# Hybrid MoBA / RWKV-7 layer on one core: GpSimd idle in the first stage, a fifth tile from the unnormed x, a shorter first chain step, a split last tile, a new tile order

## The chip, the cores and the metric

The kernel runs on 1 core of one Trainium2 chip. The metric is device microseconds of one execution: the median of 3 runs of the kernel before is 571.07 us (570.91 to 571.47).

## What is computed

One layer of a decoder trunk, in float32, for 512 tokens of width 1024. Cut to what matters here:

```python
u = rms_norm(x, g_pre)                 # x * rsqrt(mean(x*x) + 1e-6) * g_pre, a factor per token
cols = u @ w_in                        # 49 tiles of 128 columns: q k v z of branch A, r k v z of branch B,
                                       # decay and in-context-rate inputs, 16 tiles of two merge gates
y_a = block_attention(q, k, v, rel_bias) * silu(z_A)
state = 0                              # branch B, per head a 64x64 state; a scan over the tokens
state = state * w_t + (state @ a_t) b_t' + v_t k_t';  y_t = state @ r_t
y_b = (group_norm(y) + bonus) * silu(z_B)
merged = sigmoid(g_A) * (y_a @ p_a) + sigmoid(g_B) * (y_b @ p_b)
h = x + rms_norm(merged @ w_out, g_post)
out = h + sigmoid(h @ w_ple_gate) * (p @ w_ple_up)
```

The norm's factor belongs to a token, so a tile of `cols` may be made from x times g_pre and multiplied by the factor afterwards.

## The kernel before

Tokens lie along the free dimension (T = 512), features on the 128 partitions. A product "tile" is 128 output columns by 512 tokens: 8 blocks of the contraction, and for each block 3 matmuls (`product`, `mm3`), since both sides are split into a high and a low part: high by high, high weight by low activation, low weight by high activation. The high part is a rounding copy on ScalarE (ACT), the low part a subtraction on VectorE (DVE). So a tile is 24 matmuls on TensorE (PE) and, for its weights, one ACT copy `whi` and one DVE subtraction `wlo` of 128x1024. Two buffers hold split weights: a tile's weights can be split once the tile two places ahead has been multiplied.

**First stage.** x comes in four pieces of 128x1024 (two token halves h by two feature halves q), between them the weights of the first tiles. `x_split` makes `xh` (ACT) and `xl` (DVE) from x times g_pre, 128x256 at a time. `first_tiles` makes four tiles from these, before the norm is known: k0 and r0 (PSUM tiles named s) in the order k0 half 0, r0 half 0, k0 half 1, r0 half 1, then v0 (named y) and the tile of the decay and rate inputs (named c). `first_out` multiplies them by the norm's factor. Meanwhile `squares` sums x*x: half 0 on GpSimd (POOL), half 1 with ACT's Square and DVE's additions; `pre_norm` turns the sums (`rms`) into the factor by four one-column matmuls (g<-ones,rms), a short DVE sequence and four matmuls that spread it (g<-cst,rb); then it makes `uf` (DVE) for the 8 feature blocks, and `norm_split` makes `u_hi` (ACT) and `u_lo`, the latter on POOL or DVE, whichever the planner takes to be free earlier.

**Filling tiles.** The other 45 column tiles are made by `fill` from `u_hi` and `u_lo` in the order of the table FILL, into two PSUM buffers (pp); `evacuate` empties them in the same order. Between their matmuls a planner (`Plan.run`) places the work of branch B (`rwkv`, `inverse`, `chain`, `post`) and the attention. It keeps a modelled time for each engine, takes the engine whose next item can start first, and breaks ties by ranks (RC, RR_, RI, RP and so on). The instructions of each engine run in the order in which the planner issued them.

**The chain.** `chain(s)` steps 8 times (c = 0 to 7) through the state `SV` of two tiles of heads. A step's output in PSUM tile y is a product of `W2` with the step's new values plus, on top, a product of `W1` with the state. At c = 0 the state is zero (memset).

**The end.** `gate_out` multiplies h by `w_ple_gate`, 8 tiles w0 to w7; `gate_evac` takes each through ACT's Tanh and two DVE instructions to an output DMA. The last tile, w7, is made in two halves of 256 tokens, each in its own PSUM buffer.

Of the kernel before, what the change touches and what calls it, by code (L numbers as in the profile page):

```python
# [32 lines left out]
OP = mybir.AluOpType  # L33
# [8 lines left out]
GN_EPS = 64e-5  # L42
DECAY = math.exp(-0.5)
FILL = """
Z0 Q0 V0 r1 K0 v1 z0 g0 k1 g1 r2 g2 k2 g3 Q1 Z1 K1 z1 V1 g4 v2 r3 v3
g5 k3 V2 Z2 g6 K2 g7 Q2 g8 g9 g10 g11 V3 Z3 K3 Q3 z2 g12 z3 g13 g14 g15
"""

LAST = "o0 o1 o5 o2 o6 o3 o7 o4 w2 w0 w1 w3 w4 w5 w6 w7"
# [7 lines left out]
SQ = 0.1  # L57
SAME = 0.03
URGENT = 5
RC, RR_, RI, RP, RA, RE, RW = 10, 9, 6, 2, 8, 10, 11  # L60
WR, WA, WC = 0.0, 0.0, 0.0

VEC = {}
# [263 lines left out]
def hybrid_kernel(ctx: ExitStack, tc, xT, pT, wu, wda, wmain, wpab, wout, wpg, vec_in, cst_in, oneh, relb, wupa,  # L327
# [13 lines left out]
    def bank(tag="g", bufs=2):  # L341
        return psum.tile([128, 512], F32, tag=tag, name=tag, bufs=bufs)
# [87 lines left out]

    FULL = slice(0, T)
    HALF = slice(0, T // 2), slice(T // 2, T)

    def product(name, ps, mh, ml, kts, cols=FULL, done=True, pace=None):

# [269 lines left out]
    def squares(h, sq):  # L705

        for q in range(2):
            ks = slice(4 * q, 4 * q + 4)
            yield ("wait", f"dx{h}{q}")
            if h:  # L710
                yield "A"
                act.activation(sq[:, ks], x_sb[:, h, ks], AF.Square)
            else:
                yield "G"
                pool.tensor_tensor(sq[:, ks], x_sb[:, h, ks], x_sb[:, h, ks], op=OP.mult)
        e = dve if h else pool
        for w in (4, 2):
            yield e.key
            e.tensor_tensor(sq[:, 0:w], sq[:, 0:w], sq[:, w:2 * w], op=OP.add)
        yield e.key  # L720
        e.tensor_tensor(rms[:, HALF[h]], sq[:, 0], sq[:, 1], op=OP.add)
        plan.mark(f"sum{h}")

    def pre_norm():
# [34 lines left out]
    def norm_split(kt, uf):  # L759
        yield "A"  # L760
        act.activation(u_hi[:, kt, :], uf, AF.Copy)
        e = pool if plan.t["G"] + 0.7 < plan.t["D"] else dve
        yield e.key
        e.tensor_tensor(u_lo[:, kt, :], uf, u_hi[:, kt, :].bitcast(F32), op=OP.subtract)
        plan.mark(f"u{kt}")

    def bias_lines():
# [25 lines left out]
    def statics():  # L793

        nonlocal po_, rw, W1, W2, AT32, SV, Zm, reset
        for m in ["wa", "lines", "consts"] + [f"u{k}" for k in range(8)]:
            yield ("wait", m)
        start_stack.close()
        po_ = rw_stack.enter_context(tc.tile_pool(name="post", bufs=1))
        rw = chain_stack.enter_context(tc.tile_pool(name="rwkv", bufs=1))  # L800
        W1 = rw.tile([128, 2, NCH, 4, C], F32, name="W1")
        W2 = rw.tile([128, 2, NCH, 2, 128], F32, name="W2")
        AT32 = rw.tile([128, 2, NCH, 128], F32, name="AT32")
        SV = rw.tile([128, 2, NCH, 2, 2, C], F32, name="SV")
        Zm = [rw.tile([128, NCH, 128], F16, name=f"Z{i}") for i in range(5)]
        reset = rw.tile([128, NCH, 65], F16, name="reset")
        plan.mark("open")
        yield "G"
        pool.memset(reset, 1.0)
        pool.memset(reset[:, :, 0], 0.0)  # L810
        pool.memset(reset[:, :, 33], 0.0)
        plan.mark("reset")
        pool.memset(SV[lo_, :, 0, 0, 0, :], 0.0)
        pool.memset(SV[hi_, :, 0, 1, 0, :], 0.0)
        for p in range(2):
            pool.memset(W1[hi_, p, :, 1, :], 0.0)
# [9 lines left out]
    def fill(kinds):  # L826
        for i, (w, j) in enumerate(kinds):
            if w in "krv" and j >= BUFS[w + "b"]:
                yield ("wait", f"done{w}{j - BUFS[w + 'b']}")
            if w == "z":  # L830
                yield ("wait", f"post{j - 2}" if j >= 2 else "open")
            if w in "QKVZ":
                yield ("wait", f"attn{j - 1}" if j else "usedfirst2")
            if i >= 2:
                yield ("wait", f"ev{i - 2}")
            ps = bank("pp", 2)
            yield from product(f"{w}{j}", ps, u_hi, u_lo, K8, pace=lambda k: f"u{k}")
            plan.spawn(evacuate(i, w, j, ps), 0.0, RE)
        plan.mark("filled")

    def evacuate(i, w, j, ps):
        if i:
            yield ("wait", f"ev{i - 1}")
        yield "A"
        if w in "krv":
            d, off = {"k": (KK, 4), "r": (RR, 0), "v": (VV, 8)}[w]
            d[j] = krv.tile([128, T], F32, tag=w + "b", name=w + "b", bufs=BUFS[w + "b"])
            yield from shift_mix(ps, off + j, d[j])
        elif w == "z":
            z = tmp("z", "zt")  # L850
            yield from shift_mix(ps, 12 + j, z)
            th = ZZ[j] = po_.tile([128, T], F32, tag="zb", name="zb", bufs=2)
            yield "A"
            act.activation(th, z, AF.Tanh, scale=0.5)
            yield "D"
            dve.scalar_tensor_tensor(th, th, 1.0, z, op0=OP.add, op1=OP.mult)
        elif w == "Q":
            q = QS[j] = at.tile([128, 2, T], F32R, tag="qs", name="qs")
            for h, a, b in ((0, lo_, hi_), (1, hi_, lo_)):
                yield "A"  # L860
                act.activation(q[a, h, :], ps[a], AF.Copy, scale=-0.125)
                yield "D"
                dve.scalar_tensor_tensor(q[b, h, :], ps[a], -0.125, q[a, h, :].bitcast(F32), op0=OP.mult,
                                         op1=OP.subtract)
        elif w == "K":
            kh = KH[j] = at.tile([128, 2, T], F32R, tag="kh", name="kh")
            kl = KL[j] = at.tile([128, 2, T], F32R, tag="kl", name="kl")
            for h, a, b in ((0, lo_, hi_), (1, hi_, lo_)):
                yield "A"
                act.activation(kh[a, h, :], ps[a], AF.Copy)  # L870
                act.activation(kh[b, h, :], ps[a], AF.Copy)
                yield "D"
                dve.tensor_tensor(kl[a, h, :], ps[a], kh[a, h, :].bitcast(F32), op=OP.subtract)
                yield "A"
                act.activation(kl[b, h, :], kl[a, h, :].bitcast(F32), AF.Copy)
        elif w == "V":
            vc = tmp("vc", "zt")
            act.activation(vc, ps, AF.Copy)
            VT[j] = at.tile([128, 4, 128], F32, tag="vt", name="vt")
            yield "P"  # L880
            for tt in range(4):
                s = slice(tt * 128, tt * 128 + 128)
                pe.transpose(ps[:, s], vc[:, s], ident)
            yield "A"
            act.activation(VT[j].rearrange("p a b -> p (a b)"), ps, AF.Copy)
        elif w == "Z":
            th = ZA[j] = at.tile([128, T], F32, tag="za", name="za")
            act.activation(th, ps, AF.Tanh, scale=0.5)
            yield "D"
            dve.scalar_tensor_tensor(th, th, 1.0, ps, op0=OP.add, op1=OP.mult)  # L890
        elif w == "g":
            gs = at.tile([128, T], F32, tag="est", name="gst")
            act.activation(gs, ps, AF.Tanh, scale=0.5)
            sp.dma_start(g_dram[:, j, :], gs)
        plan.mark(f"ev{i}")
        plan.mark(f"{w}{j}")
# [282 lines left out]
    def chain(s):  # L1179
# [8 lines left out]
        for c in range(NCH):  # L1188
# [33 lines left out]
            if c % 4 == 0:  # L1222
                yb = bank("y", 1).rearrange("p (a c b) -> p a c b", a=2, b=C)
            for p in two:
                pe.matmul(yb[lo_, p, c % 4], W2[:, p, c, 0, 0:64], SV[:, p, c, 0, 1, :], start=True, stop=False)
                pe.matmul(yb[hi_, p, c % 4], W2[:, p, c, 1, 0:64], SV[:, p, c, 1, 1, :], start=True, stop=False)
                pe.matmul(yb[lo_, p, c % 4], W1[:, p, c, 1, :], SV[:, p, c, 0, 0, :], start=False, stop=True)
                pe.matmul(yb[hi_, p, c % 4], W1[:, p, c, 2, :], SV[:, p, c, 1, 0, :], start=False, stop=True)
            if c % 4 == 3:
                plan.spawn(outputs(s, c, yb, Y), 0.0, RR_, WR)  # L1230
            plan.cur.now = now
# [346 lines left out]
    def gate_out():  # L1578
# [14 lines left out]
            plan.spawn(gate_evac(n, FULL, ps[n]), 0.1)  # L1593
        for n in range(3, 8):
            yield ("wait", f"w{n - 4}" if n > 3 else "e3")
            for c in HALF if n == 7 else (FULL,):
                p = bank("g", 2) if n % 4 == 3 else bank(("c", "s0", "s1")[n % 4], 1)
                yield from product(f"w{n}", p, F["hi"], F["lo"], K8, c, c != HALF[0])
                plan.spawn(gate_evac(n, c, p), 0.1)

    def gate_evac(n, c, ps):
# [64 lines left out]
```

## Time and profile before

| | |
|---|---|
| median of 3 runs | 571.07 us |
| the profiled execution | 570.33 us |
| its span | 568.5 us |
| PE busy | 555.5 us, 98% of the span |
| PE weight load busy | 450.2 us, 79% |
| DVE busy | 418.1 us, 74% |
| ACT busy | 290.1 us, 51% |
| POOL busy | 18.3 us, 3% |
| chain that ended last | PE 84%, DVE 11%, ACT 2% |
| mean granted TensorE clock | 0.994 of full |

The span is from the first to the last instruction; the profiled execution's own time has 1.8 us around it. Times in rows count from the span's start. Matmuls overlap one another: the distance between two starts is what one costs in a stream, not its duration. A plain float32 matmul runs as two passes, and each pass is a record; the split products (float32r) have one.

### The profile page before, as it was taken

The numbers are of one execution on the slowest core, as the hardware profiler recorded it, in microseconds if no ns is written. First come the engines' busy times: TensorE is split into PE (matmuls) and PEld (weight loads), VectorE is DVE, ScalarE is ACT, GpSimd is POOL, SyncE is SP. The second block draws the span as 40 slices with busy tenths as digits, with TensorE's granted clock in tenths as the row PEclk, the third lists the DMA queues.
The fourth block names the chain that finished last, engine by engine and source line by source line (L and its number), as shares of the span: only waits on it lengthen the run. The fifth ranks groups of instructions, "written<-read, shape, count | busy, mean of one in ns | idle before, by whom it ended". The sixth has DMA issues, their size and how long they took to land.

```text
span 568.5 us, 10221 instructions
## 1 busy us (share of the span) xinstructions
PE 555.5 (98%) x3983; PEld 450.2 (79%) x3983; DVE 418.1 (74%) x922; ACT 290.1 (51%) x568; POOL 18.3 (3%) x26
## 2 busy tenths in 40 slices
PE   5999999999999999999999999999999999999997
PEld 2986788877777777777778777777888898999886
DVE  6988679799677777879988865589856666488623
ACT  7535683763355665464855434754533255543311
POOL 6121100000000000000000000000000000000000
PEclk9799999999999999999999999999999999999999
DMA  8322523123421204332222331124565557702201
GB/s 303 132 71 86 176 93 111 56 75 126 145 80 71 93 1 139 118 121 96 80 91 92 112 112 52 62 86 143 199 200 208 187 185 270 247 10 66 93 38 55
DMA packets 27704, 66.56 MB, mean 117 GB/s; under 512 B 2911, under 2 KB 7519, under 8 KB 27656
## 3 DMA queue, kind: packets, MB, share of 16 engines
q1 hardware_dynamic: 27656, 65.91, 34.0%
q8 instruction: 31, 0.51, 0.4%
q14 instruction: 17, 0.14, 0.1%
HBM read 56.71 MB, written 11.82 MB: 121 GB/s over the span
## 4 chain that ended last, share of the span: by engine, by line
PE 84%; DVE 11%; ACT 2%; issue 1%; DMA 1%; ACTq 0%; DVEq 0%; SPq 0%
PE pp L294 47%; PE s L294 14%; PE g L294 11%; PE c L294 7%; PE y L294 5%; DVE wlo L294 2%; DVE xl L294 1%; DVE u_lo L294 1%; DMA xg<-xT 1%; DMA yf<-yB_dram 1%; DVE uf L294 1%; DVE Ep L294 1%; DVE ts L294 0%; DVE var L294 0%; DVE h_lo L294 0%
## 5 line engine op out<-in xcount | busy, mean ns | idle before, releaser
L294 PE MATMUL pp<-u_hi,whi 128*128 128x512 f32 x360 | 145.9, 405 | 0.8 <-DVE za L294 0.6
L294 PE MATMUL pp<-u_lo,whi 128*128 128x512 f32 x360 | 145.0, 403 | 0.0
L294 PE MATMUL pp<-u_hi,wlo 128*128 128x512 f32 x360 | 144.6, 402 | 0.0
L294 ACT ACTIVATE whi<-raw 128x1024 fp32r<-128x1024 f32 (+1 forms) x86 | 71.5, 846 | 73.2 <-PE pp L294 55.4
L294 DVE TENSOR_TENSOR wlo<-raw,whi 128x1024 fp32r<-128x1024 f32 (+1 forms) x86 | 81.5, 960 | 25.1 <-ACT whi L294 24.6
L294 PEld LDWEIGHTS pp<-u_hi,whi 128*128 128x128 f32 x360 | 67.7, 188 | 15.2 <-issue 2.0
L294 PEld LDWEIGHTS pp<-u_lo,whi 128*128 128x128 f32 x360 | 67.8, 188 | 12.8 <-issue 0.6
L294 PEld LDWEIGHTS pp<-u_hi,wlo 128*128 128x128 f32 x360 | 67.8, 188 | 12.6 <-issue 0.2
L294 ACT ACTIVATE P<-P,sml 128x128 f32<-128x128 f32 (+3 forms) x32 | 17.7, 554 | 9.1 <-DVE sml L294 9.1
L294 DVE SCALAR_TENSOR_TENSOR SV<-c,D,sd 64x64 f32<-64x64 f32 x56 | 15.9, 283 | 8.2 <-PE c L294 6.7
L294 ACT ACTIVATE Xt<-y 128x512 f16<-128x512 f32 x20 | 11.9, 593 | 17.0 <-PE y L294 16.7
L294 ACT ACTIVATE sd<-SV,D 64x64 f32<-64x64 f32 x56 | 19.3, 344 | 1.1
L294 DVE TENSOR_TENSOR Z<-c,lvl 128x512 f16<-128x512 f32 x20 | 13.7, 687 | 5.4 <-PE c L294 5.3
L294 PEld LDWEIGHTS c<-SV,W 128*64 128x64 f32 x240 | 9.6, 136 | 9.7 <-issue 4.8
L294 PE MATMUL pp<-m_hi,whi 128*128 128x512 f32 (+1 forms) x48 | 17.0, 354 | 0.0
L294 PE MATMUL pp<-m_lo,whi 128*128 128x512 f32 (+1 forms) x48 | 17.0, 354 | 0.0
L294 PE MATMUL pp<-m_hi,wlo 128*128 128x512 f32 (+1 forms) x48 | 17.0, 354 | 0.0
L294 DVE SCALAR_TENSOR_TENSOR xl<-xg,xh 128x256 fp32r<-128x256 f32 x16 | 13.0, 876 | 5.0 <-ACT xh L294 5.0
L294 DVE CUSTOM_DVE_ANT_0 P<-s,bt 128x128 f32<-128x128 f32 (+3 forms) x32 | 14.4, 487 | 1.7 <-PE s L294 1.4
L294 DVE TENSOR_SCALAR SV<-c 64x128 f32<-64x128 f32 x30 | 8.6, 288 | 9.5 <-PE c L294 5.9
L294 PE MATMUL s<-xl,whi 128*128 128x256 f32 x32 | 10.8, 338 | 3.8 <-DVE xl L294 3.8
L294 DVE SCALAR_TENSOR_TENSOR t<-gb,pp 128x512 f32<-128x512 f32 (+1 forms) x8 | 5.2, 654 | 12.5 <-PE pp L294 12.5
(366 smaller groups left out, 1246.5 us busy)
## 6 DMA issues: line engine op xcount, KB each, us to landing
raw<-wmain SPq DMA_DIRECT2D x48, 512.0 KB, 3.3
g_dram<-gst SPq DMA_DIRECT2D x16, 256.0 KB, 2.0
raw<-wpab SPq DMA_DIRECT2D x8, 512.0 KB, 3.3
raw<-wout SPq DMA_DIRECT2D x8, 512.0 KB, 3.5
raw<-wpg SPq DMA_DIRECT2D x8, 512.0 KB, 5.8
bb_dram<-b_dram SPq DMA_DIRECT2D x4, 640.0 KB, 5.9
bt<-bb_dram SPq DMA_DIRECT2D x8, 256.0 KB, 3.6
ga<-g_dram SPq DMA_DIRECT2D x8, 256.0 KB, 3.8
```

The lines of the kernel that those rows point to most:

```text
L294: r = f(out, *args, **kw)
```

## The change

`squares` puts both halves on ACT (Square) and DVE (additions); `norm_split` puts every `u_lo` on DVE. POOL's first work after the start is now the memsets at 50-odd us. The first filling tile, g0, is made from `xh` and `xl`; its `evacuate` multiplies by the factor (`rms`) on DVE before the Tanh. The chain's first step leaves out the products with the zero state. The last tile goes in pieces of 256, 128 and 128 tokens, the two narrow ones in one PSUM buffer. FILL has a new order, RP goes from 2 to 7.

```diff
 FILL = """
-Z0 Q0 V0 r1 K0 v1 z0 g0 k1 g1 r2 g2 k2 g3 Q1 Z1 K1 z1 V1 g4 v2 r3 v3
-g5 k3 V2 Z2 g6 K2 g7 Q2 g8 g9 g10 g11 V3 Z3 K3 Q3 z2 g12 z3 g13 g14 g15
+g0 r1 Z0 Q0 V0 K0 z0 v1 g1 k1 z1 r2 g2 g3 k2 g4 Z1 K1 Q1 V1 v2 r3 v3
+g5 k3 V2 Z2 g6 K2 Q2 g7 g8 g9 g10 V3 K3 Q3 g11 Z3 z2 z3 g12 g13 g14 g15
 """
-RC, RR_, RI, RP, RA, RE, RW = 10, 9, 6, 2, 8, 10, 11
+RC, RR_, RI, RP, RA, RE, RW = 10, 9, 6, 7, 8, 10, 11
...
+    ENDS = HALF[0], slice(T // 2, 3 * T // 4), slice(3 * T // 4, T)
...
     def squares(h, sq):
         for q in range(2):
-            if h:
-                yield "A"
-                act.activation(sq[:, ks], x_sb[:, h, ks], AF.Square)
-            else:
-                yield "G"
-                pool.tensor_tensor(sq[:, ks], x_sb[:, h, ks], x_sb[:, h, ks], op=OP.mult)
-        e = dve if h else pool
+            yield "A"
+            act.activation(sq[:, ks], x_sb[:, h, ks], AF.Square)
         for w in (4, 2):
-            yield e.key
-            e.tensor_tensor(sq[:, 0:w], sq[:, 0:w], sq[:, w:2 * w], op=OP.add)
+            yield "D"
+            dve.tensor_tensor(sq[:, 0:w], sq[:, 0:w], sq[:, w:2 * w], op=OP.add)
...
     def norm_split(kt, uf):
-        e = pool if plan.t["G"] + 0.7 < plan.t["D"] else dve
-        yield e.key
-        e.tensor_tensor(u_lo[:, kt, :], uf, u_hi[:, kt, :].bitcast(F32), op=OP.subtract)
+        yield "D"
+        dve.tensor_tensor(u_lo[:, kt, :], uf, u_hi[:, kt, :].bitcast(F32), op=OP.subtract)
...
     def fill(kinds):
-            yield from product(f"{w}{j}", ps, u_hi, u_lo, K8, pace=lambda k: f"u{k}")
+            if i:
+                yield from product(f"{w}{j}", ps, u_hi, u_lo, K8, pace=lambda k: f"u{k}")
+            else:
+                yield ("wait", "usedfirst3")
+                yield from product(f"{w}{j}", ps, xh, xl, K8)
...
     def evacuate(i, w, j, ps):
+        else:
+            for k in range(6):
+                yield ("wait", f"u{k}")
+            gs = at.tile([128, T], F32, tag="est", name="gst")
+            yield "D"
+            dve.tensor_tensor(gs, ps, rms, op=OP.mult)
+            ps = gs
...
     def chain(s):
-                pe.matmul(yb[lo_, p, c % 4], W2[:, p, c, 0, 0:64], SV[:, p, c, 0, 1, :], start=True, stop=False)
-                pe.matmul(yb[hi_, p, c % 4], W2[:, p, c, 1, 0:64], SV[:, p, c, 1, 1, :], start=True, stop=False)
-                pe.matmul(yb[lo_, p, c % 4], W1[:, p, c, 1, :], SV[:, p, c, 0, 0, :], start=False, stop=True)
-                pe.matmul(yb[hi_, p, c % 4], W1[:, p, c, 2, :], SV[:, p, c, 1, 0, :], start=False, stop=True)
+                for rows, h in ((lo_, 0), (hi_, 1)):
+                    pe.matmul(yb[rows, p, c % 4], W2[:, p, c, h, 0:64], SV[:, p, c, h, 1, :], start=True, stop=c == 0)
+                for rows, h in ((lo_, 0), (hi_, 1)) if c else ():
+                    pe.matmul(yb[rows, p, c % 4], W1[:, p, c, 1 + h, :], SV[:, p, c, h, 0, :], start=False, stop=True)
...
     def gate_out():
-            for c in HALF if n == 7 else (FULL,):
-                p = bank("g", 2) if n % 4 == 3 else bank(("c", "s0", "s1")[n % 4], 1)
-                yield from product(f"w{n}", p, F["hi"], F["lo"], K8, c, c != HALF[0])
+            for c in ENDS if n == 7 else (FULL,):
+                if c != ENDS[2]:
+                    p = bank("g", 2) if n % 4 == 3 else bank(("c", "s0", "s1")[n % 4], 1)
+                yield from product(f"w{n}", p, F["hi"], F["lo"], K8, c, c.stop == T)
                 plan.spawn(gate_evac(n, c, p), 0.1)
```

What the change moves, at the three places that the prediction speaks of. First DVE, from the end of the small parameter preparations (`oka`) to the norm's first instruction (`ms4`); `sq` are the squared halves, `wlo` a low weight part. Before, then now:

```order
L294 TENSOR_SCALAR oka_79<-hka_78 128x4
L294 TENSOR_TENSOR sq_141<-sq_141 128x1024
L294 TENSOR_TENSOR sq_141<-sq_141 128x512
L294 TENSOR_TENSOR rms_113<-sq_141 128x256
L294 TENSOR_TENSOR wlo_306<-raw_225,whi_305 128x1024
L294 TENSOR_SCALAR ms4_368<-g_139 128x4
```

```order
L294 TENSOR_SCALAR oka_79<-hka_78 128x4
L294 TENSOR_TENSOR sq_140<-sq_140 128x1024
L294 TENSOR_TENSOR sq_140<-sq_140 128x512
L294 TENSOR_TENSOR rms_113<-sq_140 128x256
L294 TENSOR_TENSOR sq_141<-sq_141 128x1024
L294 TENSOR_TENSOR sq_141<-sq_141 128x512
L294 TENSOR_TENSOR rms_113<-sq_141 128x256
L294 TENSOR_TENSOR wlo_302<-raw_223,whi_301 128x1024
L294 TENSOR_SCALAR ms4_381<-g_139 128x4
```

Half 0's three additions have come to DVE, ahead of those of half 1.

Second PE, from the end of the fourth tile (c) into the first filling tile (pp). Before, then now:

```order
L294 MATMUL c<-xl,shi 128x512
L294 MATMUL c<-xh,slo 128x512
L294 MATMUL pp<-u_hi,whi 128x512 [waits Activation_49]
L294 MATMUL pp<-u_lo,whi 128x512 [waits Pool_49]
L294 MATMUL pp<-u_hi,wlo 128x512
```

```order
L294 MATMUL c<-xl,shi 128x512
L294 MATMUL c<-xh,slo 128x512
L294 MATMUL pp<-xh,whi 128x512 [waits Activation_49]
L294 MATMUL pp<-xl,whi 128x512
L294 MATMUL pp<-xh,wlo 128x512
```

The 24 matmuls behind the fourth tile read x instead of u; the first matmul that waits for u comes one tile later, and none waits for POOL.

Third PE, in the last tile (w7, in PSUM tile g). Before, its 48 matmuls are 256 wide up to the program's end; now 24 are so, and 48 are narrow. The end before; then, of the change, the place where the narrow ones begin, and the place where the third piece begins (its first matmul is the fourth row of the last fence):

```order
L294 MATMUL g<-h_lo,whi 128x256
L294 MATMUL g<-h_hi,wlo 128x256
L294 MATMUL g<-h_hi,whi 128x256
L294 MATMUL g<-h_lo,whi 128x256
L294 MATMUL g<-h_hi,wlo 128x256
L1661 UNCONDITIONAL_BRANCH
```

```order
L294 MATMUL g<-h_hi,whi 128x256
L294 MATMUL g<-h_lo,whi 128x256
L294 MATMUL g<-h_hi,wlo 128x256
L294 MATMUL g<-h_hi,whi 128x128
L294 MATMUL g<-h_lo,whi 128x128
L294 MATMUL g<-h_hi,wlo 128x128
```

```order
L294 MATMUL g<-h_hi,whi 128x128
L294 MATMUL g<-h_lo,whi 128x128
L294 MATMUL g<-h_hi,wlo 128x128
L294 MATMUL g<-h_hi,whi 128x128
L294 MATMUL g<-h_lo,whi 128x128
L294 MATMUL g<-h_hi,wlo 128x128 [waits Activation_49]
```

The number of matmuls in the last tile goes from 48 to 72, and its third piece has a wait for ACT at its third matmul.

## Rows read from the trace of the kernel before

**Rows 1.** Busy time by stretch: us, busy us (instructions) by engine, clock, DMA.
```profile
10.00:15.00 5.00, 1.63 (x6) 1.13 (x6) 5.00 (x3) 5.00 (x15) 4.77 (x3) 0.83 1.03 396
15.00:20.00 5.00, 4.73 (x21) 4.58 (x22) 5.00 (x13) 3.60 (x8) 0.79 (x1) 0.50 0.59 198
...
60.00:500.00 440.00, 439.12 (x3331) 352.31 (x3330) 330.22 (x737) 234.51 (x445) 0.00 (x0) 1.00 0.36 122
```

**Rows 2.** PE in order of time, first stage: start us, us, instruction.
```profile
6.57 0.38 PE L294 MATMUL s<-xh,whi 128*128 128x256 f32 x1 [0.37 <-ACT whi L294]
...
13.85 0.58 PE L294 MATMUL s<-xl,whi 128*128 128x256 f32 x1 [1.89 <-DVE xl L294]
...
26.64 0.28 PE L294 MATMUL s<-xl,whi 128*128 128x256 f32 x1
26.76 0.28 PE L294 MATMUL s<-xh,wlo 128*128 128x256 f32 x1
...
39.39 0.40 PE L294 MATMUL c<-xl,shi 128*128 128x512 f32 x1
39.62 0.39 PE L294 MATMUL c<-xh,slo 128*128 128x512 f32 x1
```

**Rows 3.** DVE in order of time, 9 to 40 us.
```profile
9.18 6.91 DVE L294 SCALAR_TENSOR_TENSOR xl<-xg,xh 128x256 fp32r<-128x256 f32 x4
...
17.35 3.25 DVE L294 SCALAR_TENSOR_TENSOR xl<-xg,xh 128x256 fp32r<-128x256 f32 x8
...
23.63 1.94 DVE L294 TENSOR_TENSOR sq<-sq 128x1024 f32<-128x1024 f32 x2
...
25.95 1.22 DVE L294 TENSOR_TENSOR wlo<-raw,whi 128x1024 fp32r<-128x1024 f32 x1
...
34.47 2.72 DVE L294 SCALAR_TENSOR_TENSOR uf<-xg,g 128x512 f32<-128x512 f32 x4 [0.38 <-PE g L294]
37.23 2.46 DVE L294 TENSOR_TENSOR u_lo<-uf,u_hi 128x512 fp32r<-128x512 f32 x2
```

**Rows 4.** ACT in order of time, 10 to 19 us.
```profile
10.96 3.29 ACT L294 ACTIVATE xh<-xg 128x256 fp32r<-128x256 f32 x8
...
16.60 2.00 ACT L294 ACTIVATE sq<-xg 128x1024 f32<-128x1024 f32 x2
```

**Rows 5.** POOL in order of time, 8 to 15 us.
```profile
8.17 2.84 POOL L294 TENSOR_TENSOR sq<-xg 128x1024 f32<-128x1024 f32 x1 [1.72 <-DMA xg<-xT]
11.09 3.85 POOL L294 TENSOR_TENSOR sq<-sq 128x1024 f32<-128x1024 f32 x2
```

**Rows 6.** PE, a stall behind DVE at 53 us.
```profile
53.19 0.47 PE L294 MATMUL pp<-u_hi,whi 128*128 128x512 f32 x1 [0.56 <-DVE za L294]
```

**Rows 7.** PE in a chain step: eight output matmuls (two passes each), then large ones.
```profile
359.57 0.64 PE L294 MATMUL y<-SV,W 128*64 128x64 f32 x16
360.13 0.50 PE L294 MATMUL pp<-u_hi,whi 128*128 128x512 f32 x1
360.47 0.39 PE L294 MATMUL pp<-u_lo,whi 128*128 128x512 f32 x1
```

**Rows 8.** PE, narrow matmuls: one column, then 128 columns.
```profile
28.97 0.95 PE L294 MATMUL g<-ones,rms 128*128 128x1 f32 x8
...
79.22 0.22 PE L294 MATMUL s<-kh,qs 128*128 128x128 f32 x1
79.28 0.27 PE L294 MATMUL s<-kl,qs 128*128 128x128 f32 x1
79.39 0.33 PE L294 MATMUL s<-kh,qs 128*128 128x256 f32 x1
```

**Rows 9.** The end on PE, ACT and DVE, last half tile.
```profile
564.10 0.28 PE L294 MATMUL g<-h_hi,wlo 128*128 128x256 f32 x1
...
564.41 0.38 ACT L294 ACTIVATE th<-g 128x256 f32<-128x256 f32 x1 [2.34 <-PE g L294]
...
565.28 0.42 DVE L294 SCALAR_TENSOR_TENSOR x_sb<-th,x_sb 128x256 f32<-128x256 f32 x1
```

More of the change, by code (lines that the diff above doesn't have):

```diff
@@ L709, in squares @@
             yield ("wait", f"dx{h}{q}")
-            if h:
-                yield "A"
-                act.activation(sq[:, ks], x_sb[:, h, ks], AF.Square)
-            else:
-                yield "G"
-                pool.tensor_tensor(sq[:, ks], x_sb[:, h, ks], x_sb[:, h, ks], op=OP.mult)
-        e = dve if h else pool
+            yield "A"
+            act.activation(sq[:, ks], x_sb[:, h, ks], AF.Square)
         for w in (4, 2):
-            yield e.key
-            e.tensor_tensor(sq[:, 0:w], sq[:, 0:w], sq[:, w:2 * w], op=OP.add)
-        yield e.key
-        e.tensor_tensor(rms[:, HALF[h]], sq[:, 0], sq[:, 1], op=OP.add)
+            yield "D"
+            dve.tensor_tensor(sq[:, 0:w], sq[:, 0:w], sq[:, w:2 * w], op=OP.add)
+        yield "D"
+        dve.tensor_tensor(rms[:, HALF[h]], sq[:, 0], sq[:, 1], op=OP.add)
         plan.mark(f"sum{h}")
@@ L761, in norm_split @@
         act.activation(u_hi[:, kt, :], uf, AF.Copy)
-        e = pool if plan.t["G"] + 0.7 < plan.t["D"] else dve
-        yield e.key
-        e.tensor_tensor(u_lo[:, kt, :], uf, u_hi[:, kt, :].bitcast(F32), op=OP.subtract)
+        yield "D"
+        dve.tensor_tensor(u_lo[:, kt, :], uf, u_hi[:, kt, :].bitcast(F32), op=OP.subtract)
         plan.mark(f"u{kt}")
@@ L795, in statics @@
         nonlocal po_, rw, W1, W2, AT32, SV, Zm, reset
-        for m in ["wa", "lines", "consts"] + [f"u{k}" for k in range(8)]:
+        for m in ["wa", "lines", "consts", "ev0"] + [f"u{k}" for k in range(8)]:
             yield ("wait", m)
@@ L843, in evacuate @@
             yield ("wait", f"ev{i - 1}")
+        else:
+            assert w == "g"
+            for k in range(6):
+                yield ("wait", f"u{k}")
+            gs = at.tile([128, T], F32, tag="est", name="gst")
+            yield "D"
+            dve.tensor_tensor(gs, ps, rms, op=OP.mult)
+            ps = gs
         yield "A"
@@ L891, in evacuate @@
         elif w == "g":
-            gs = at.tile([128, T], F32, tag="est", name="gst")
+            gs = at.tile([128, T], F32, tag="est", name="gst") if i else ps
             act.activation(gs, ps, AF.Tanh, scale=0.5)
```

## Prediction

> **What bounds the kernel now.** I read the busy time by stretch first. From 60 to 500 us PE is busy for 439.12 of 440 us [rows 1]: in that stretch the order of the work, DVE and ACT can give back 0.9 us at most, and whatever puts PE ahead at 60 us stays, as long as the others keep up. What PE loses, it loses ahead of 60 us and behind its last matmul. The same view shows where: from 10 to 15 us PE is busy for 1.63 of 5 us, and from 15 to 20 us it is busy, but at a granted clock of 0.50, the lower level (1.2 GHz), after a stretch in which it mostly stood still.
>
> PE's own rows say what it waits for: the first stage's product begins at 6.57 us, and one of its gaps, 1.89 us, ends with DVE's `xl` [rows 2]. Starts of the 256-wide matmuls are 0.12 us apart when nothing waits (26.64, 26.76) and those of the 512-wide ones 0.23 us (39.39, 39.62) [rows 2]. The 96 matmuls on the first two tiles, 6.57 to 26.88 us, take 20.3 us where 96 x 0.12 = 11.5 us would do: 8.8 us are lost there.
>
> DVE's rows say why. Four `xl` from 9.18 us take 6.91 us, and eight of the same shape from 17.35 us take 3.25 us [rows 3], 1.73 against 0.41 us each. In the slow ones POOL runs `sq` (8.17 for 2.84 us, 11.09 for 3.85 us [rows 5], 4.77 of the 5 us from 10 to 15 [rows 1]); in the fast ones it stands still. ACT goes on at 0.41 us each through the same time (eight `xh` in 3.29 us from 10.96 us [rows 4]), so x has arrived.
>
> **The change part by part, against the profiled execution (570.33 us).**
>
> *POOL idle, first stage.* The four `xl` that start at 9.18 us end at 9.18 + 4 x 0.41 = 10.8 instead of 16.1 us. PE's first quarter (24 matmuls) then ends at 11.1, and the other three follow at 3 x 24 x 0.12 = 8.6 us: the last `xl`, one 0.41 us step behind ACT's last `xh` (14.25 us), is there before PE wants it. That is 19.7 instead of 26.9 us, a gain of 7.2 us; the `xl` ahead of 9.18 run beside POOL too, so the start may come 0.6 us sooner. Ends: nothing, if POOL is not the cause, and 8.8 us, the whole loss. I take 7.5 us, near the upper end, because the fast rows are the same instruction.
>
> *What POOL did must go elsewhere.* ACT gets two more squares, 2.0 us, behind those at 16.60 us [rows 4], and ends them at 20.6 us. DVE gets the additions of half 0, 1.94 and about 0.4 us [rows 3]. From the last `xl` to the additions it needs 23.63 - 20.60 = 3.0 us, now 14.7 to 17.7; half 0 is added from 18.6 to 21.0 us, half 1 to 23.4 us. PE asks for the sums after 7 of the 8 blocks of its third tile, at 19.4 + 21 x 0.235 = 24.3 us: hidden by 0.9 us, and if the cover goes each us late is a us of PE. The four `u_lo` that come from POOL cost DVE nothing net: two `u_lo` beside POOL take 2.46 us [rows 3], and alone I estimate 0.61 us each, half of the 1.22 us of the 1024-wide `wlo` [rows 3], so four take 2.44 us.
>
> *The fifth tile from x.* Its 24 matmuls are only moved. Without it PE, 7.5 us early, would run into the norm: its fourth tile ends at 39.62 + 0.23 [rows 2] before, 32.4 us now, and the first `uf`, which follows the spreading matmuls, starts at 34.47 us before [rows 3], 5.4 us ahead of PE's first use of u, and at about 19.4 + 33 x 0.235 + 0.95 + 1.0 = 29.1 us now, only 3.3 us ahead. With the tile (24 x 0.235 = 5.6 us) PE reaches u at 38.0 us, 8.9 us behind the first `uf`: covered. The extra multiplication `gst` is 0.65 us on DVE, off PE's path. Z0's weights now wait for g0 to leave their buffer, so their ACT copy stands between the sixth and seventh `u_hi`, 1.1 us; PE wants those blocks 4 us later. Next late would be the seventh `u_lo`, by my count 0.9 us ahead of PE.
>
> *Tile order.* By the order's table PE's sequence has 158 changes from large matmuls to small groups and back instead of 154. The first large matmul behind a group takes 0.34 us to the next start instead of 0.23 [rows 7]: 4 x 0.1 = +0.4 us. The stall of 0.56 us on `za` at 53.19 us [rows 6] goes: Z0 is the third tile now, its buffer is wanted at the fifth, and DVE empties it 2 us ahead: -0.6 us. RP decides ties only: nothing.
>
> *First chain step.* It loses 4 products in each of two chains, 8 instructions, 16 passes. Sixteen passes take 360.13 - 359.57 = 0.56 us [rows 7]: -0.6 us.
>
> *The last tile.* The pieces carry the same columns, but 24 matmuls more. What does a 128-wide one cost? After one, the next start comes 0.06 or 0.11 us later (79.22, 79.28, 79.39), and even eight passes with one column take 0.95 us, 0.12 each [rows 8]: each has its own weight load, and the load seems to set the pace. Lower end 0.06, upper end 0.12; I take 0.11, because a long row of narrow ones is nearest to the one-column rows. The tile's narrow half then takes 48 x 0.11 = 5.4 instead of 24 x 0.113 = 2.7 us: +2.7 us (ends +0.2 and +3.0), and nothing covers it, PE being last. The third piece's new wait is for ACT's Tanh on the second, which shares its PSUM buffer: a Tanh of some 0.3 us less the two matmuls issued ahead of it, with the hand-overs +0.4 us (nothing to 0.6). PSUM — Partial Sum Buffer, section "PSUM bank collisions raise a hardware error", in the Trainium skill has software guard PSUM by bank, not by address, which is the form of this wait; no run here shows it yet. Behind PE's last matmul the path is Tanh 0.38 and two DVE instructions of 0.42 us [rows 9], then the output. ACT's slope from 256 to 1024 columns is (1.00 - 0.38) / 768 = 0.8 ns, DVE's from 256 to 512 (0.68 - 0.42) / 256 = 1 ns, so 128 fewer columns give 0.1 + 2 x 0.13, and the smaller output some 0.1: -0.5 us. Together +2.6 us.
>
> The Trainium skill, TensorE: Matmul & The Clock Gate, section "Back-to-back issue gap", speaks of about 81 ns for each 128-wide matmul with its weight load. By it the narrow half would take 3.9 us and the sum would be 1.5 us lower; I go by the 0.11 of the rows here.
>
> **Sum:** -7.5 - 0.6 + 0.4 - 0.6 + 2.6 = -5.7 us, 564.6 for the profiled execution. It lies 0.7 us under the median of the runs shown, so I predict 565.3 us, with 564.0 to 567.0 as this case's own range.
>
> **The rivals.**
> - *POOL is not what slows `xl`; the arriving data is.* For it: DMA is at a share of 1.03 in the slow stretch and 0.59 in the next [rows 1]. Against it: ACT reads the same x at full pace in that stretch, and POOL's rows coincide. Then the 7.5 us do not come, and the added squares and split tile remain: 571.07 - 0.6 + 0.4 - 0.6 + 2.6 = 572.9 us. It decides wherever the first stage gains less than 1.8 us: slower. Chance 0.07.
> - *The clock still falls.* The lower level covers about 6.7 us (0.17 x 5 / 0.5 of the one stretch, all of the next [rows 1]) and costs half of it, 3.3 us, if PE is dense there. Against it: from 10.8 us on PE has no gap of the kind that stood ahead of the fall. 568.6 us, chance 0.08.
> - *PE's lead is partly given back after 40 us.* DVE starts its u stage 5 us earlier and carries `gst` and Z0's split on top, PE is 7.5 us early; a buffer emptied late costs 0.56 us each time [rows 6], and five such make 568.1 us. Against it: DVE is idle for a quarter of 60 to 500 us [rows 1] and catches up. Chance 0.10.
> - *Narrow matmuls are cheap,* 0.06 us each, the lower end: 2.5 us less, 562.8 us. For it the 0.06 between 79.22 and 79.28, against it the 0.95 us for eight [rows 8]. The rule of 81 ns lies between, and would give 563.8 us from 565.3. Chance 0.12 for both.
>
> **How the numbers follow.** The forecast has 0.63. A measurement of this kernel can tell about 0.2%, 1.1 us, from no change. Faster takes the forecast and the last three rivals but for their worst tails: 0.90; slower the first: 0.07; the rest, 0.03, is the same. The range 562.6 to 568.9 us holds all but the first rival and the tails of the others.
>
> **What would show it.** Right: `xl` at 0.41 us throughout, the third tile (y) starting near 19.4 instead of 26.9 us at full clock, u first used near 38 us, 60 to 500 us as dense as now; the 48 narrow matmuls 0.11 us apart, one gap of about 0.4 us at the third piece. Wrong: `xl` still over 1 us, a clock of 0.50 in the first 20 us, PE waits of half a us between 40 and 110 us, or narrow matmuls under 0.08 us apart.

## The result, and the profile after

The changed kernel takes 564.29 us (median of 4 runs, 564.17 to 565.14), the kernel before beside it 570.99 us (4 runs, 570.60 to 571.47): a ratio of 0.9885, interval 0.9868 to 0.9903. The forecast was 565.3 us, range 562.6 to 568.9. The profiled execution took 564.17 us, its span 562.4 us; before these were 570.33 and 568.5 us.

The first lines of the page after: busy time, PE's slices, and the granted clock in 40 slices.

```profile
PE 554.3 (99%) x3991; PEld 450.9 (80%) x3991; DVE 414.4 (74%) x931; ACT 292.4 (52%) x572; POOL 3.9 (1%) x17
...
PE   8999999999999999999999999999999999999997
...
PEclk9999999999999999999999999999999999999999
```

PE has 8 records more than before (3991 against 3983): 24 narrow matmuls more, 16 passes of the chain's first step less. The clock has no dip left.

Busy time by stretch, after (columns as in [rows 1]: us; busy us and instructions of PE, PEld, DVE, ACT, POOL; clock; DMA share; GB/s):

```profile
10.00:15.00 5.00, 5.00 (x43) 5.00 (x42) 5.00 (x14) 5.00 (x15) 0.00 (x0) 1.00 1.04 397
15.00:20.00 5.00, 5.00 (x41) 4.89 (x40) 4.29 (x16) 5.00 (x10) 0.00 (x0) 1.00 0.77 297
60.00:500.00 440.00, 438.69 (x3345) 353.62 (x3343) 333.14 (x748) 237.17 (x458) 0.00 (x0) 1.00 0.36 118
```

From 10 to 15 us PE is busy all the time, where it was for 1.63 of 5 us [rows 1], at the same DMA share (1.04 against 1.03). From 60 to 500 us it is as dense as before.

DVE in order of time, after:

```profile
4.96 1.68 DVE L294 SCALAR_TENSOR_TENSOR xl<-xg,xh 128x256 fp32r<-128x256 f32 x4 [4.96 <-ACT xh L294]
...
8.61 1.68 DVE L294 SCALAR_TENSOR_TENSOR xl<-xg,xh 128x256 fp32r<-128x256 f32 x4 [0.63 <-ACT xh L294]
...
11.55 3.25 DVE L294 SCALAR_TENSOR_TENSOR xl<-xg,xh 128x256 fp32r<-128x256 f32 x8
...
20.93 1.94 DVE L294 TENSOR_TENSOR sq<-sq 128x1024 f32<-128x1024 f32 x2
22.91 0.42 DVE L294 TENSOR_TENSOR rms<-sq 128x256 f32<-128x256 f32 x1
```

Every `xl` takes 0.41 or 0.42 us; the four that took 6.91 us [rows 3] take 1.68. PE in order of time, after, first stage and then the narrow matmuls of the end:

```profile
6.54 0.39 PE L294 MATMUL s<-xh,whi 128*128 128x256 f32 x1 [0.69 <-ACT whi L294]
...
19.33 0.39 PE L294 MATMUL y<-xh,qs 128*128 128x512 f32 x1
...
24.25 0.95 PE L294 MATMUL g<-ones,rms 128*128 128x1 f32 x8
...
32.33 0.39 PE L294 MATMUL pp<-xh,whi 128*128 128x512 f32 x1
...
37.93 0.39 PE L294 MATMUL pp<-u_hi,whi 128*128 128x512 f32 x1
...
555.46 0.27 PE L294 MATMUL g<-h_hi,whi 128*128 128x128 f32 x1
555.57 0.28 PE L294 MATMUL g<-h_lo,whi 128*128 128x128 f32 x1
556.22 0.33 PE L294 MATMUL g<-h_hi,wlo 128*128 128x128 f32 x1 [0.37 <-ACT th L294]
...
558.61 0.28 PE L294 MATMUL g<-h_hi,wlo 128*128 128x128 f32 x1
```

The third tile starts at 19.33 instead of 26.88 us: 7.55 us gained. The sums (DVE's last addition ends at 23.33) are there 0.9 us before PE asks at 24.25. PE reaches u at 37.93 us, and no matmul of that tile has a wait. PE's lead over the kernel before is 8.65 us at the last matmul of the filling tiles (it starts at 407.41 against 416.06 us) and the same at the norm of the output (its one wait in both, 503.9 and 512.6 us). Then the last tile costs: at PE's last matmul the lead is 5.48 us (558.89 against 564.37), and behind it 3.5 instead of 4.1 us remain.

### The profile page after: what moved, and what is told of

Read it like the earlier page. It is cut to its first block, busy times and chain, and to the rows that moved or that the text cites. A ratio compares the mean times of both kernels' runs of the same rounds, so it can differ in the third digit from the quotient of the medians.

```text
span 562.4 us, 10228 instructions
## 1 busy us (share of the span) xinstructions
PE 554.3 (99%) x3991; PEld 450.9 (80%) x3991; DVE 414.4 (74%) x931; ACT 292.4 (52%) x572; POOL 3.9 (1%) x17
## 4 chain that ended last, share of the span: by engine, by line
PE 91%; ACT 3%; DVE 3%; DMA 1%; issue 1%; SPq 0%; DVEq 0%; ACTq 0%
PE pp L294 52%; PE s L294 13%; PE g L294 12%; PE c L294 8%; PE y L294 5%; DMA xg<-xT 1%; ACT SV L294 1%; ACT whi L294 1%; DVE Ep L294 1%; ACT kh L294 0%; DVE wlo L294 0%; DVE h_lo L294 0%; ACT Xt L294 0%; DVE SV L294 0%; ACT En L294 0%
## 5 line engine op out<-in xcount | busy, mean ns | idle before, releaser
L294 PE MATMUL pp<-u_lo,whi 128*128 128x512 f32 x352 | 142.3, 404 | 0.0
L294 PE MATMUL pp<-u_hi,whi 128*128 128x512 f32 x352 | 142.2, 404 | 0.0
L294 PE MATMUL pp<-u_hi,wlo 128*128 128x512 f32 x352 | 141.8, 403 | 0.0
L294 PEld LDWEIGHTS pp<-u_hi,wlo 128*128 128x128 f32 x352 | 66.3, 188 | 13.1 <-issue 1.6
L294 PEld LDWEIGHTS pp<-u_hi,whi 128*128 128x128 f32 x352 | 66.2, 188 | 13.0 <-issue 0.5
L294 PEld LDWEIGHTS pp<-u_lo,whi 128*128 128x128 f32 x352 | 66.3, 188 | 11.6 <-issue 0.2
L294 PE MATMUL c<-SV,W 128*64 128x64 f32 x240 | 13.6, 234 | 0.2 <-DVE SV L294 0.2
L294 DVE TENSOR_SCALAR P<-P,sml 128x128 f32<-128x128 f32 (+3 forms) x32 | 12.4, 387 | 1.1
```

The source lines that it names most:

```text
L294: r = f(out, *args, **kw)
```

## Experiments

All times are medians with the kernel before beside them, which took 570.1 to 570.4 us in these comparisons.

| kernel | us (lowest to highest) | ratio to before, interval |
|---|---|---|
| GpSimd idle alone | 565.24 (564.30 to 565.76) | 0.9909, 0.9893 to 0.9926 |
| ... and the fifth tile | 566.89 (564.59 to 567.69) | 0.9936, 0.9921 to 0.9952 |
| ... and the new order, RP = 7 | 565.32 (564.85 to 566.72) | 0.9919, 0.9904 to 0.9934 |
| ... and the chain's step (= changed, halves at the end) | 561.73 (561.65 to 562.45) | 0.9853, 0.9837 to 0.9870 |
| the same with RP = 2 | 561.37 (561.36 to 561.45) | 0.9845, 0.9832 to 0.9859 |
| new order and RP = 7, nothing else | 575.32 (574.74 to 575.50) | 1.0087, 1.0074 to 1.0101 |
| changed, third piece in its own buffer | 563.65 (563.49 to 563.68) | 0.9883, 0.9868 to 0.9897 |
| changed, squares back on GpSimd | 584.22 (582.84 to 585.31) | 1.0243, 1.0221 to 1.0264 |
| ... with the changed order kept | 572.11 (571.45 to 573.00) | 1.0035, 1.0022 to 1.0048 |
| changed, GpSimd multiplies a scratch | 572.38 (571.91 to 573.20) | 1.0039, 1.0027 to 1.0051 |
| changed, GpSimd copies a scratch | 568.28 (567.04 to 568.94) | 0.9964, 0.9951 to 0.9978 |
| changed, GpSimd fills a scratch | 564.53 (564.36 to 565.05) | 0.9902, 0.9889 to 0.9914 |

### Is it GpSimd that slows `xl`?

Squares back on GpSimd:

```diff
-            yield "A"
-            act.activation(sq[:, ks], x_sb[:, h, ks], AF.Square)
+            if h:
+                yield "A"
+                act.activation(sq[:, ks], x_sb[:, h, ks], AF.Square)
+            else:
+                yield "G"
+                pool.tensor_tensor(sq[:, ks], x_sb[:, h, ks], x_sb[:, h, ks], op=OP.mult)
+        e = dve if h else pool
...
```

> The changed kernel with half 0's squares and their additions on GpSimd again; all else stays as changed. Theory (GpSimd's work slows VectorE's xl): xl beside it at 1.7 us instead of 0.41, the third tile starts near 27 us instead of 19.3, the clock falls to the lower level, 564.3 + 7.5 = 571.8 us. Rival (the gain came from the new order of the tiles and the fifth tile from x, not from GpSimd): 564.3 to 566 us.

It took 584.22 us, 12 us over the theory. PE's filling starts only 7.7 us late, as expected (the second filling tile starts at 45.65 against 37.93), but the planner, told of another first stage, had written another order behind it. Busy time by stretch, then two lines of PE's waits (us in total, times, longest us):

```profile
60.00:500.00 440.00, 432.58 (x3228) 343.70 (x3227) 325.38 (x717) 234.01 (x445) 2.01 (x4) 0.99 0.36 120
```

```profile
PE pp L294 <- DVE qs L294: 3.0, 1, 3.0
PE s L294 <- ACT kl L294: 1.7, 2, 1.3
```

PE stands still for 7.4 us of that stretch, in the changed kernel for 1.3. So this undoing mixes two things. The next one issues the squares and additions on GpSimd but prices them as ScalarE's and VectorE's, so that the rest keeps the changed order (PE's 3991 records have the same sequence in both traces):

```diff
+    class Squares:
+        def activation(self, out, a, f):
+            nc.gpsimd.tensor_tensor(out, a, a, op=OP.mult)
+    like_act, like_dve = Engine(Squares(), plan, "A"), Engine(nc.gpsimd, plan, "D")
...
-            act.activation(sq[:, ks], x_sb[:, h, ks], AF.Square)
+            (act if h else like_act).activation(sq[:, ks], x_sb[:, h, ks], AF.Square)
+        e = dve if h else like_dve
...
```

> The changed kernel with half 0's squares and additions on GpSimd, but the planner is told that they are still on ScalarE and VectorE, so every other instruction keeps its place in the changed kernel's order. Theory (the squares cost 7.5 us, and the 12 us more of the first undoing came from the order that the planner then chose): 564.0 + 7.5 = 571.5 us, the third tile near 27 us, no more waits than now from 60 to 500 us. Rival (a late first stage spoils everything behind it): 580 us or more.

572.11 us, the theory's 571.5 within 0.6. PE's first matmul of the third tile, in the timeline, and the busy time by stretch:

```profile
27.30 0.39 PE L294 MATMUL y<-xh,qs 128*128 128x512 f32 x1
```

```profile
10.00:15.00 5.00, 2.95 (x11) 2.07 (x9) 5.00 (x3) 5.00 (x15) 4.76 (x4) 0.50 1.04 398
15.00:20.00 5.00, 4.82 (x21) 4.66 (x22) 5.00 (x13) 3.60 (x8) 0.72 (x1) 0.50 0.58 202
```

The third tile is 7.97 us late, the clock is at its lower level (0.50, 1.2 GHz) again behind the gaps, and the kernel is 7.8 us slower: the first stage's gain is GpSimd's, and none of it is regained later.

What about GpSimd does it? Three kernels give it work on a scratch tile that nobody else touches: the loop has ten multiplications, ten copies or 24 memsets.

```diff
...
+            if h == 0 and q == 0:
+                g = nc.gpsimd
+                g.tensor_tensor(scr[:, 0:64], x_sb[:, 0, 0, 0:64], x_sb[:, 0, 0, 0:64], op=OP.mult)
+                for _ in range(10):
+                    g.tensor_tensor(scr[:, 64:T], scr[:, 64:T], scr[:, 64:T], op=OP.mult)
```

> The changed kernel with ten added multiplications on GpSimd in the first stage, of a scratch tile of its own with itself (128x448 each, behind one small product that reads x); nobody reads the scratch. Theory (GpSimd and VectorE get in each other's way whatever they read): xl near 1.7 us beside it, the third tile at 26 to 27 us, 570 to 572 us. Rival (they collide because both read x): xl stays at 0.41 us, 564.3 us.

> As with the ten multiplications on GpSimd's own scratch, but with ten plain copies of the scratch onto itself: one operand is read, not two. Theory (it is GpSimd's reading that holds VectorE up): xl well over 0.41 us beside the copies, 567 to 572 us. Rival (it takes two read operands; one is as harmless as the memsets): xl at 0.41 us, 564.3 to 565 us.

> The changed kernel with 24 memsets of a scratch tile (128x448) on GpSimd in the first stage, behind one small product that reads x. Memsets read nothing. Theory (what collides is GpSimd's reading): xl stays at 0.41 us but for the first, 564.3 to 565 us. Rival (any running GpSimd instruction holds VectorE up): xl near 1.7 us, 570 to 572 us.

GpSimd and VectorE in order of time: with the multiplications,

```profile
4.93 10.59 POOL L717 TENSOR_TENSOR scr<-scr 128x448 f32<-128x448 f32 x10
...
5.10 4.25 DVE L294 SCALAR_TENSOR_TENSOR xl<-xg,xh 128x256 fp32r<-128x256 f32 x4 [5.10 <-ACT xh L294]
9.28 4.37 DVE L294 TENSOR_TENSOR wlo<-raw,whi 128x256 fp32r<-128x256 f32 x4
```

with the copies,

```profile
5.10 6.82 POOL L717 COPY scr<-scr 128x448 f32<-128x448 f32 x10
...
5.29 2.73 DVE L294 SCALAR_TENSOR_TENSOR xl<-xg,xh 128x256 fp32r<-128x256 f32 x4 [5.29 <-ACT xh L294]
7.95 2.86 DVE L294 TENSOR_TENSOR wlo<-raw,whi 128x256 fp32r<-128x256 f32 x4
```

and with the memsets:

```profile
4.94 12.68 POOL L717 MEMSET scr<- 128x448 f32 x24
...
5.14 1.68 DVE L294 SCALAR_TENSOR_TENSOR xl<-xg,xh 128x256 fp32r<-128x256 f32 x4 [5.14 <-ACT xh L294]
...
8.71 1.69 DVE L294 SCALAR_TENSOR_TENSOR xl<-xg,xh 128x256 fp32r<-128x256 f32 x4 [0.55 <-ACT xh L294]
```

The copies cost 4.0 us and the multiplications 8.1 us of the whole; 24 memsets, longer on GpSimd than either, cost 0.2 us, which is nothing that can be told. So what slows `xl` is not that both engines read x, nor that GpSimd runs at all: beside the two kinds of work that read, of one operand or of two, it is slow, and beside the one that only writes it is not. SBUF — State Buffer, section "Who interferes with whom", in the Trainium skill says this: a VectorE instruction with two SBUF inputs contends with a GpSimd instruction that reads SBUF, not with one that only writes it. `xl` and `wlo` have two such inputs; the traces agree on both halves of the rule.

VectorE's side of it can be read from the kernel before, where GpSimd makes some of the `u_lo`:

```profile
35.96 2.58 POOL L294 TENSOR_TENSOR u_lo<-uf,u_hi 128x512 fp32r<-128x512 f32 x2 [20.16 <-ACT u_hi L294]
...
37.23 1.86 DVE L294 TENSOR_TENSOR u_lo<-uf,u_hi 128x512 fp32r<-128x512 f32 x1
...
39.02 0.68 DVE L294 TENSOR_TENSOR u_lo<-uf,u_hi 128x512 fp32r<-128x512 f32 x1
```

VectorE's `u_lo`, with two inputs in SBUF, takes 1.86 us beside GpSimd and 0.68 without it. `uf` has one tile in SBUF (x) and one in PSUM (g), and its four from 34.47 us take 0.68 us each [rows 3], though GpSimd reads from 35.96 us on.

### What the fifth tile is worth

GpSimd idle in the kernel before, nothing else: the edits of the change in `squares` and `norm_split`.

```diff
+            yield "A"
+            act.activation(sq[:, ks], x_sb[:, h, ks], AF.Square)
...
+        yield "D"
+        dve.tensor_tensor(u_lo[:, kt, :], uf, u_hi[:, kt, :].bitcast(F32), op=OP.subtract)
```

> The kernel before with one part of the change alone: the squares, their additions and every u_lo leave GpSimd; the first filling tile still waits for u. Theory (without the fifth tile from x PE runs into the norm): the third tile starts near 19.4 us and the fourth ends at 32.4 us, but VectorE delivers a block of u (uf 0.68, u_lo 0.65 us) every 1.35 us from 29.1 us on, the last near 40 us, so PE ends its first tile of u near 40.6 instead of 38.0 us and 2.6 of the 7.5 us are lost: 571.0 - 7.5 + 2.6 = 566.1 us. Rival (the fifth tile brings nothing, u is there in time): 571.0 - 7.5 = 563.5 us. Second rival (GpSimd is not the cause): 571 us.

565.24 us, 0.9 under the theory's 566.1 and 1.7 over the rival's 563.5. PE's waits in its first tile of u, in order of time:

```profile
36.27 0.49 PE L294 MATMUL pp<-u_hi,whi 128*128 128x512 f32 x1 [0.55 <-ACT u_hi L294]
37.00 0.50 PE L294 MATMUL pp<-u_lo,whi 128*128 128x512 f32 x1 [0.23 <-DVE u_lo L294]
...
38.98 0.50 PE L294 MATMUL pp<-u_hi,whi 128*128 128x512 f32 x1 [0.54 <-ACT u_hi L294]
39.70 0.50 PE L294 MATMUL pp<-u_lo,whi 128*128 128x512 f32 x1 [0.23 <-DVE u_lo L294]
```

Here PE does run into the norm. Now the fifth tile from x is added, with g0 at the head of the old table:

```diff
-Z0 Q0 V0 r1 K0 v1 z0 g0 k1 g1 r2 g2 k2 g3 Q1 Z1 K1 z1 V1 g4 v2 r3 v3
+g0 Z0 Q0 V0 r1 K0 v1 z0 k1 g1 r2 g2 k2 g3 Q1 Z1 K1 z1 V1 g4 v2 r3 v3
...
+                yield from product(f"{w}{j}", ps, xh, xl, K8)
```

> GpSimd idle and the fifth tile from x in the kernel before: the first gate tile is put at the head of the old tile order and made from x; the last tile in halves and the chain's first step stay as before. Theory (the fifth tile covers the norm, which cost GpSimd idle alone 2.3 us in its first tile of u): 565.2 - 2.3 = 562.9 us. Rival (the cover brings nothing, since PE is held up later anyway): 565.2 us.

A miss: 566.89 us, no gain at all. The cover works (the second filling tile starts at 38.09 instead of 41.80 us, 3.7 us sooner, the fifth at 56.60 instead of 61.55), but then comes this, on PE and on DVE in order of time:

```profile
118.80 0.38 PE L294 MATMUL s<-cst,P 128*128 128x128 f32 x2
122.36 0.91 PE L294 MATMUL s<-P,vt 128*64 128x128 f32 x6 [3.18 <-DVE P L294]
...
118.55 1.24 DVE L294 TENSOR_TENSOR_SCAN Ep<-reset,En 128x520 f32<-128x520 f16 x1
...
120.39 1.22 DVE L294 TENSOR_TENSOR wlo<-raw,whi 128x1024 fp32r<-128x1024 f32 x1
121.52 0.69 DVE L294 COPY P<-s 128x512 f32<-128x512 f32 x1
```

The attention's copy of P stands behind a scan and a weight split on DVE, and PE waits 3.18 us for it; behind that wait the clock from 120 to 200 us is 0.96. This is the forecast's third rival (the lead given back after 40 us), at about its price (2.8 us), but in one wait instead of five, and not in the changed kernel. So the cover is shown, by PE's lead at the second and the fifth filling tile; what the fifth tile is worth in the whole time is not, for nothing was tried that takes it out of the changed kernel alone.

### The tile order and the chain's step

To that kernel the new order and RP = 7 are added; then both go into the kernel before, with nothing else (the edit shown); then RP goes back to 2 in the changed kernel with halves at the end.

```diff
-Z0 Q0 V0 r1 K0 v1 z0 g0 k1 g1 r2 g2 k2 g3 Q1 Z1 K1 z1 V1 g4 v2 r3 v3
-g5 k3 V2 Z2 g6 K2 g7 Q2 g8 g9 g10 g11 V3 Z3 K3 Q3 z2 g12 z3 g13 g14 g15
+g0 r1 Z0 Q0 V0 K0 z0 v1 g1 k1 z1 r2 g2 g3 k2 g4 Z1 K1 Q1 V1 v2 r3 v3
+g5 k3 V2 Z2 g6 K2 Q2 g7 g8 g9 g10 V3 K3 Q3 g11 Z3 z2 z3 g12 g13 g14 g15
...
-RC, RR_, RI, RP, RA, RE, RW = 10, 9, 6, 2, 8, 10, 11
+RC, RR_, RI, RP, RA, RE, RW = 10, 9, 6, 7, 8, 10, 11
```

> The kernel with GpSimd idle and the fifth tile from x, now with the changed kernel's tile order and rank RP; the last tile in halves and the chain's first step stay as before. Theory (the old tile order asked for the attention's P too early, one wait of 3.2 us at 122 us and a lower clock behind it; the new order doesn't): that wait is gone, 561.7 us of the halves version + 0.6 for the chain's first step = 562.3 us. Rival (the chain's shorter step is what removed the wait): a wait of 2 us or more stays, 564.5 us or more.

> The kernel before with nothing but the new tile order and RP; its first gate tile comes first and is made from u. Theory (the order is worth what the prediction gave it, -0.2 us, whatever the first stage does): 570.0 us. Rival (an order fits the lead that it was chosen for; with PE 7.5 us later the waits fall elsewhere): 571.5 us or more, with waits of a us between 60 and 500 us.

> The changed kernel with its last tile in halves and RP back at 2. Theory (RP decides ties only): 561.7 us, within 0.6. Rival (the ranks steer the order as much as the table does): a wait of a us or more appears between 60 and 500 us, 563 us or more.

The new order takes the wait at 122 us away, and the time goes down by 1.6 us only, to 565.32: of PE's waits one is new, with `X`.

```profile
282.26 0.39 PE L294 MATMUL c<-Xt,AT 128*128 128x64 f16 x8 [1.45 <-ACT X L294]
```

The difference between this kernel and the changed one with halves is the chain's first step, 8 instructions; it makes 565.32 - 561.73 = 3.6 us, not 0.6. Leaving them out also moves the planner's times, and PE's order is another in many places behind it; the wait of 1.45 us at 282 us and one of 0.51 us at 265 us are gone in the other order. These 2.0 us and the 0.6 of the instructions themselves leave 1.0 us whose place is not shown. Neither the theory nor the rival had it so: the wait at 122 us was the order's, and another took its place until the chain's step moved it.

In the kernel before, the new order with RP = 7 makes 575.32 us, 5.2 us slower (the rival): from 60 to 500 us PE stands still for 4.4 us, where it did for 0.9. Its longest wait there:

```profile
86.59 0.33 PE L294 MATMUL s<-kl,qs 128*128 128x128 f32 x1 [2.14 <-ACT kl L294]
```

RP at 2 gives 561.37 us, 0.36 us less than with 7. The two were measured on different occasions and their intervals overlap, so this is too little to tell; RP at 7 gains nothing, as predicted, though it does move instructions.

### The last tile

Back in two halves, each in its own buffer:

```diff
-    ENDS = HALF[0], slice(T // 2, 3 * T // 4), slice(3 * T // 4, T)
+    ENDS = HALF
...
-                if c != ENDS[2]:
+                if True:
```

> The changed kernel with its last tile made as before: two halves of 256 tokens, each in its own PSUM buffer. Theory (a matmul costs its weight load, however narrow): the 48 narrow matmuls took 48 x 0.11 + 0.54 us of waiting = 5.8 us, and 24 of 256 columns take 2.7 us; the tail behind PE grows by 0.6 us. So 564.3 - 3.1 + 0.6 = 561.8 us, faster than both kernels. Rival (the pieces pay for themselves: what stands behind PE's last matmul, Tanh, VectorE and the output, bounds the end): 564.3 us or more.

561.73 us: 2.6 us under the changed kernel, as expected, and the ranges of the two do not meet. And three pieces, the third in its own buffer:

```diff
-                if c != ENDS[2]:
+                if c == ENDS[2]:
+                    p = bank("c", 1)
+                else:
...
```

> The changed kernel with the third piece of the last tile in a PSUM buffer of its own, where it shared the second's. Theory (PE waits there for ScalarE to have read the second piece out of the shared buffer): the wait of 0.54 us goes, the 48 narrow matmuls stand 0.11 us apart throughout, 564.3 - 0.5 = 563.8 us. Rival (the wait is not the shared buffer's, or what it frees is lost behind PE): the gap stays, or the time stays at 564.3 us.

563.65 us, 0.64 us under the changed kernel. PE in order of time at the place of the wait:

```profile
555.26 0.28 PE L294 MATMUL g<-h_hi,wlo 128*128 128x128 f32 x1
555.37 0.27 PE L294 MATMUL c<-h_hi,whi 128*128 128x128 f32 x1
555.48 0.28 PE L294 MATMUL c<-h_lo,whi 128*128 128x128 f32 x1
555.59 0.27 PE L294 MATMUL c<-h_hi,wlo 128*128 128x128 f32 x1
```

The gap of 0.65 us between two starts has become 0.11, so it was the shared buffer's: the pieces lie in different columns of it, and the wait held all the same. That is the form which the Trainium skill gives such a guard (PSUM — Partial Sum Buffer, section "PSUM bank collisions raise a hardware error": by bank, not by address). The 48 narrow matmuls stand 0.11 us apart throughout, but for the first gap of 0.06. So halving the width from 256 to 128 columns saves PE nothing per matmul (0.113 against 0.111 us), and the price of the finer split is its 24 more matmuls. The section "Back-to-back issue gap" of TensorE: Matmul & The Clock Gate in the Trainium skill gives about 81 ns for each 128-wide matmul with its weight load. The trace differs: 0.11 us here.

## Why the prediction was right, and where it was not

- **POOL idle.** Predicted -7.5 us, measured -7.55 at the third tile; the undoing with the order kept costs 7.8 us. So the cause was right; that it is GpSimd's reading, and not its running, the prediction did not say. The first rival (arriving data) falls: the DMA share is the same. So does the second: with PE dense the clock did not fall.
- **Moved work.** The sums are ready 0.9 us ahead of PE, as counted, and no wait shows in the u stage. The reading behind the price of `u_lo` was off: of the two in [rows 3] only the first ran beside POOL (1.86 us), and alone two take 1.28 to 1.35 us in the changed kernel, where 1.22 was estimated. It cost PE no wait.
- **The fifth tile.** Predicted as cover for the norm; without it PE loses 2.2 us of its lead by the end of the first tile of u (7.4 us ahead of the kernel before at the third tile, 19.45 against 26.88; 5.2 at the second filling tile's start, 41.80 against 47.03). Added by itself it brought no time, so its share of the sum is not shown.
- **Order and chain.** Predicted +0.4 - 0.6 - 0.6 = -0.8 us; the lead grew by 8.65 - 7.55 = 1.1 us. The sum stands, and the step behind it does not: order and chain were costed as local edits that hold by themselves. The runs show that neither does. The order (with RP) is +5.2 us in the kernel before, and the chain's step is -3.6 us on top of the others. Four of the re-planned kernels have a wait of 1.4 to 3.2 us between 60 and 500 us; the changed one has none over 0.3 there, which the prediction took for granted by assuming [rows 1] as dense as before. That the sum came out so near is in part luck: taken one after another, GpSimd idle, the fifth tile, the order with RP, the chain's step and the split last tile measure -4.9, +1.7, -1.6, -3.6 and +2.6 us.
- **The last tile.** Predicted +2.7 for the narrow matmuls, +0.4 for the wait, -0.5 behind PE: +2.6 us. Measured: 0.11 us each, a wait of 0.54 us, 0.6 us less behind PE; taking it all back gains 2.6 us. The fourth rival (0.06 us, or 81 ns) falls.
- **The sum.** -5.7 us predicted, -6.2 measured between the profiled executions; the forecast was 1.0 us high, of which 0.6 came from the step to the median: the profiled execution lay 0.7 us under it before, but 0.1 after.

The last tile was a loss that the forecast named, and the version without it is the fastest: 561.73 us, 0.9853 of the kernel before. With RP at 2 it is 561.37 us, not to be told from it.

Left open: which of the moved instructions makes the wait on `X`, what the fifth tile is worth in the changed order, and where the 0.3 us come from by which the lead grew beyond the sum; none was tried.

## What to carry to other kernels

Keep GpSimd away from reading while VectorE runs instructions with two SBUF inputs on the path; memsets cost nothing here. Don't split a last tile below 256 columns for a shorter tail: 128 columns cost as much as 256 here, 0.11 us, and the tail gave back 0.6 us of 3.2. And where a planner writes the order, an edit that is small or undone is a new order: keep the order fixed to measure the edit, and look for waits of a few us behind every re-planning before believing a sum of local costs.

## What the runs showed of the hardware

GpSimd and VectorE did not slow each other in proportion: where both had work in a row, they took turns, one instruction each. Beside the multiplications four `xl` take 4.25 us, 1.06 each, and ten multiplications 10.59 us, also 1.06 each; beside the copies it is 2.73 / 4 = 0.68 and 6.82 / 10 = 0.68. An `xl` that takes 0.41 us elsewhere so loses 0.65 us to each multiplication and 0.27 to each copy. The kernel before has the same pairs, GpSimd first and then VectorE:

```profile
4.55 1.89 POOL L294 TENSOR_TENSOR sq<-xg 128x1024 f32<-128x1024 f32 x1 [3.18 <-DMA xg<-xT]
...
11.09 2.42 POOL L294 TENSOR_TENSOR sq<-sq 128x1024 f32<-128x1024 f32 x1
...
15.01 0.79 POOL L294 TENSOR_TENSOR rms<-sq 128x256 f32<-128x256 f32 x1
...
7.83 1.42 DVE L294 TENSOR_TENSOR wlo<-raw,whi 128x256 fp32r<-128x256 f32 x4
...
11.21 2.58 DVE L294 SCALAR_TENSOR_TENSOR xl<-xg,xh 128x256 fp32r<-128x256 f32 x1
...
15.14 0.94 DVE L294 SCALAR_TENSOR_TENSOR xl<-xg,xh 128x256 fp32r<-128x256 f32 x1
```

Each of these two `xl` ends 0.28 us after the GpSimd instruction that started just ahead of it, so the longer that one is, the longer a single `xl` waits. The turns are not always one for one: GpSimd's `sq` that starts at 8.17 us [rows 5], with VectorE already at a row of `wlo`, leaves these at their full pace and itself takes 2.84 us, where the first `sq` took 1.89. What decides who goes first no run here shows.
